# Two-layer recurrent and attention trunk on one core: norm factors found by token and spread by TensorE, a convolution that reads the accumulators, and another order of the work

## The chip, the core and the metric

The kernel runs on one core of a Trainium2 chip. The metric is the device time of one execution in microseconds (us). The kernel before took 615.57 us as the median of three runs (612.71, 615.57 and 615.72). One more execution was profiled; it took 608.61 us.

## The reference, cut to what matters

The input is a stream x of 256 tokens with 1024 features. Two layers each add a mixer and a feed-forward network to it, and a last norm follows. Everything is float32. Ahead of each product the stream is normed and then scaled and shifted by columns that come from the vector c:

```
rmsnorm(x, g) = x * rsqrt(mean(x*x over features) + 1e-6) * g
modulate(h, shift, scale) = h * (1 + scale) + shift        # shift, scale = silu(c) @ mod_w + mod_b
layer 0: x += g_m * rglru(h);       x += g_f * swiglu(h)
layer 1: x += g_m * attention(h);   x += g_f * swiglu(h)   # keys and values from a norm of their own
out = rmsnorm(x, final_norm)
```

The recurrent mixer (rglru) multiplies h by an input matrix, runs a causal convolution of four taps over the tokens of one half of the result, forms two gates from it, scans over the tokens, multiplies by a gelu of the other half and applies an output matrix. The convolution is

```
xc[t] = conv_b + sum over k = 0..3 of conv_w[k] * x_br[t - 3 + k]     # zero ahead of the first token
```

## The kernel before

Everything stands with features on the 128 partitions and the 256 tokens along the free axis, so the stream is eight tiles of 128 x 256. A float32 product is made in one of two ways. In the split way (`gemm`, `mm3`, L383 to L389) weights and data are each cut into a rounded high part and a low rest, and three matmuls replace one; ScalarE writes the high part of a weight unit (L439) and VectorE the low part (L440). In the native way the float32 tiles are multiplied as they are, and the profile has two records for each such matmul.

**Order of the work.** Nothing is ordered by a scheduler of the compiler. `build` writes down every operation with an estimated cost, a rank (its place in the text, plus a bias of the stage, plus a bias by tile name from the tables `PRIO`), and the buffers that it reads and writes. `Plan.run` (L153 to L265) walks through time with these estimates: on each engine the operations that could start earliest are found, and of those the one of lowest rank goes next. The order on each engine's queue is fixed by that, the loads on SP's queue too. On the chip each engine then works through its queue in order and waits on semaphores.

**Buffers.** Raw weights land in four `raw` slots of 1 MB. Rows of the modulation matrices (`mr_...`, 512 KB each) land in three `mraw` slots; VectorE reduces each such tile with the row csb, which is silu(c) spread over all partitions (`mod_col`, L458 to L463). PSUM has eight `ps` slots of one bank.

**The start.** c (`crow`) is loaded into an mraw slot, spread over the partitions by a matmul with ones (L422) and sent through silu into `csb` (L424). x, the vector constants `vec`, then the modulation rows and the slices `wix` of the input matrix (12 tiles of 128 columns a slice, 768 KB) follow on SP's queue. For each of the eight feature tiles k, VectorE makes the scale and the shift column (L462, L663, L666), multiplies x by the norm factor (`normed`, L555 to L558), ScalarE forms h (L563), and TensorE runs five native tiles (L677) and seven split tiles into the accumulators `xb0` to `xb4` and `yb0`.

**A norm** (`sumsq`, L522 to L553) is called four times: n0 ahead of the recurrent mixer, f0 and f1 ahead of the feed-forward networks, n2 ahead of keys, values and queries. ScalarE squares the eight tiles (L530) and VectorE adds some of them (L539). TensorE multiplies what is left by a matrix of ones (L544), so that each partition holds the sums of all tokens: one matmul in n0, five in each of the others. ScalarE takes the root of all 256 columns (L547) and VectorE the reciprocal of all 128 x 256 elements (L552). In f0, f1 and n2 the first products run on the stream before it is normed (`unnorm`, L585 to L603), and their results are multiplied by the factor afterwards (L879, L884, L988).

**The heads** (`head_front`, L695 to L739). For each of five heads ScalarE copies the accumulator `xb` into a zero-padded tile `xpad` (L699), writes the first tap (L705), and VectorE adds three more taps for each half (L709). Then the gates are made (`ga`, L725), with sigmoid, tanh, exp and root on ScalarE. `mod_cols_pe` (L465 to L497) makes the columns sh_f0 and g_m0 with TensorE from four loads each of 1 MB (`sh_f_r`, `g_m_r`, matmuls on L477). The keys are finished on VectorE (L990).

Of the kernel before, what the change touches and what calls it, by code (L numbers as in the profile page):

```python
# [92 lines left out]
class Plan:  # L93
# [59 lines left out]
    def run(self):  # L153
# [15 lines left out]
        te, table = {"ACT": 0.6, "DVE": 0.6, "POOL": 0.57, "PE": 0.1, "SP": 1.7}, [None]  # L169
# [102 lines left out]
    "shat": 0, "gmat": 1, "win": 600, "tol": 3.6321997149340305e-16, "nn": 5, "nyh": 1, "sqpe": 4, "gnat": 5,  # L272
# [5 lines left out]
        "cps": -877, "n_st": -1, "xb": 779, "yb": 1804, "ga": -19, "sh_f_ps": -1801, "sh_f_pt": 1118, "wo": -42,  # L278
        "g_m_ps": -799, "g_m_pt": -888, "f_st": 65, "f_g": 1113, "f_p": -3, "f_d": 23, "rp": 3432, "kp": -27, "vp":
        -23, "sp": -62, "pt": -29, "op": 1946, "ao": -145, "ty": 1267,  # L280
    },
    "ACT": {
        "csb": -187, "csc": -3, "n_sq": 1636, "n_rstd": 1867, "wix_h": -609, "h_": -1591, "h_h": -1809, "sp_e":
        -1313, "sp_ln": -1887, "xpad": 3698, "i": 1175, "v": 3772, "y": 3589, "wiy_h": 897, "sh_f_row": 473, "uh":
        -144, "wout_h": 2439, "g_m_row": -3, "f_warm": 1733, "f_sq": 8, "f_rstd": 458, "f_u_f": -2634, "f_": 54,
        "f_h": -427, "f_tg": 643, "f_ah": 1225, "fb_h": 3819, "f_s": 54, "fc_h": 15, "n_warm": 300, "kv_sh": 12,
        "wk_h": 785, "kv_u_h": -2508, "hkv_": 62, "hkv_h": -8, "hq_": 28, "hq_h": -2771, "wv_h": 3001, "v_": 4134,
        "wq_h": 2113, "qT": -1187, "sm": 4131, "e": -19, "pT": 132, "oh": 731, "wo__h": -26, "f_sh": -349, "fa_h":
        -75, "f_u_h": 619, "rs": 388, "out": -1641,
    },  # L290
    "DVE": {
        "epst": -623, "ones": 162, "n_sq": -421, "n_rstd": 796, "b": 2980, "sc": 15, "sh": 330, "wix_l": -577, "n_":
        396, "h_l": -2, "sp_neg": -45, "sp_ab": -1042, "sp_ln": 730, "sp_e": 357, "sp_d": -873, "sp_z": 171, "sp_s":
        -119, "xc": 4215, "i": -1135, "wiy_l": -1247, "r": 129, "v": -1006, "sh_f_m": 291, "y": 675, "ul": 1942,
# [24 lines left out]
def build(tc, t):  # L319
    nc = tc.nc  # L320
    ctx = ExitStack()
    with ctx:
# [914 lines left out]
```

## Time and profile before

| what | us |
|---|---|
| median of three runs | 615.57 |
| lowest and highest | 612.71, 615.72 |
| the profiled execution, its own time | 608.61 |
| its span, first to last instruction | 606.8 |
| TensorE busy in the span | 585.9 |
| VectorE busy | 471.8 |
| ScalarE busy | 340.6 |

The span is the part of an execution that the trace shows; 1.8 us of the profiled execution lie around it. All rows come from this one execution. A matmul's end is modelled, so two matmuls that follow each other overlap in the rows; the distance between two starts is what one costs.

### The profile page before, as it was taken

Reading aid. Unit: us, or ns where it says so; the run is one execution under the profiler, and the core shown is the slowest. Engines: PE = TensorE matmul, PEld = TensorE weight load, DVE = VectorE, ACT = ScalarE, POOL = GpSimd, SP = SyncE. Lnnn points to the kernel's source line nnn. Section 1 sums busy time; section 2 is a strip of 40 time slices with the busy share of each in tenths; the row PEclk is TensorE's granted clock in tenths of the full one; section 3 lists DMA queues with packets and bytes.
Section 4 is the critical chain, followed back from the end, with each engine's and each line's share of the span. In section 5 each row is a group of like instructions: output and inputs, shape, how many; then the busy total and the mean of one; then the engine's idle time right before and its main releaser. Section 6 shows DMA issues by size and latency. Waiting matters only on the chain.

```text
span 606.8 us, 11423 instructions
## 1 busy us (share of the span) xinstructions
PE 585.9 (97%) x4706; PEld 563.2 (93%) x4706; DVE 471.8 (78%) x743; ACT 340.6 (56%) x509; POOL 1.2 (0%) x10
## 2 busy tenths in 40 slices
PE   3999989999999999999999999998999999999996
PEld 1999868998999999999999889998999999999996
DVE  6998788977997898788878969889997654545542
ACT  6537898718653443343336899747664444434432
POOL 0000000000000000000000000000000000000000
PEclk9999999999999999999999999999999999999999
DMA  8996999795988899798979538786686654445501
GB/s 307 353 339 239 332 355 355 278 383 224 350 312 323 336 348 323 257 334 315 377 295 357 203 143 322 282 332 245 218 306 274 214 203 165 144 144 192 191 1 70
DMA packets 33362, 162.94 MB, mean 269 GB/s; under 512 B 3700, under 2 KB 4893, under 8 KB 23966
## 3 DMA queue, kind: packets, MB, share of 16 engines
q1 hardware_dynamic: 33310, 162.21, 72.2%
q8 instruction: 37, 0.61, 0.4%
q14 instruction: 15, 0.12, 0.1%
HBM read 161.14 MB, written 1.06 MB: 267 GB/s over the span
## 4 chain that ended last, share of the span: by engine, by line
PE 63%; DMA 18%; DVE 12%; ACT 3%; issue 3%; SPq 0%; DVEq 0%; ACTq 0%
PE ps_f_p L388 11%; PE ps_f_p L387 11%; PE ps_f_p L389 11%; PE ps_f_d L388 3%; PE ps_f_d L389 3%; PE ps_f_d L387 3%; PE ps_ga L449 3%; DMA mraw_mr_sh_kv_m__2730<-in_kvmod 2%; DVE wlo_f0c_l L440 2%; DMA raw_sh_f_r<-in_modp 1%; DMA mraw_mr_g_m_m__3469<-in_mod 1%; DMA raw_wix<-in_win_x 1%; PE ps_qp L389 1%; PE ps_qp L388 1%; PE ps_qp L387 1%
## 5 line engine op out<-in xcount | busy, mean ns | idle before, releaser
L388 PE MATMUL ps_f_p<-t_f_l,whi_f0b_h 128*128 128x256 f32 x320 | 89.7, 280 | 0.0
L387 PE MATMUL ps_f_p<-t_f_h,whi_f0b_h 128*128 128x256 f32 x320 | 89.5, 280 | 0.0
L389 PE MATMUL ps_f_p<-t_f_h,wlo_f0b_l 128*128 128x256 f32 x320 | 89.3, 279 | 0.0
L389 PE MATMUL ps_f_p<-t_f_h,wlo_f1b_l 128*128 128x256 f32 x320 | 88.5, 276 | 0.0
L387 PE MATMUL ps_f_p<-t_f_h,whi_f1b_h 128*128 128x256 f32 x320 | 88.4, 276 | 0.0
L388 PE MATMUL ps_f_p<-t_f_l,whi_f1b_h 128*128 128x256 f32 x320 | 88.4, 276 | 0.0
L388 PEld LDWEIGHTS ps_f_p<-t_f_l,whi_f0b_h 128*128 128x128 f32 x320 | 60.1, 188 | 0.2 <-DVE t_f_l L568 0.2
L387 PEld LDWEIGHTS ps_f_p<-t_f_h,whi_f0b_h 128*128 128x128 f32 x320 | 60.2, 188 | 0.0
L389 PEld LDWEIGHTS ps_f_p<-t_f_h,wlo_f1b_l 128*128 128x128 f32 x320 | 60.1, 188 | 0.1
L388 PEld LDWEIGHTS ps_f_p<-t_f_l,whi_f1b_h 128*128 128x128 f32 x320 | 60.1, 188 | 0.0
L387 PEld LDWEIGHTS ps_f_p<-t_f_h,whi_f1b_h 128*128 128x128 f32 x320 | 60.1, 188 | 0.0
L389 PEld LDWEIGHTS ps_f_p<-t_f_h,wlo_f0b_l 128*128 128x128 f32 x320 | 59.8, 187 | 0.0
L440 DVE TENSOR_TENSOR wlo_f1b_l<-raw_f1b_r,whi_f1b_h 128x2048 fp32r<-128x2048 f32 x20 | 45.6, 2289 | 18.1 <-ACT whi_f1b_h L439 18.1
L439 ACT ACTIVATE whi_f1b_h<-raw_f1b_r 128x2048 fp32r<-128x2048 f32 x20 | 38.2, 1912 | 24.8 <-issue 11.9
L439 ACT ACTIVATE whi_f0b_h<-raw_f0b_r 128x2048 fp32r<-128x2048 f32 x20 | 38.2, 1910 | 21.5 <-issue 19.1
L388 PE MATMUL ps_f_d<-t_f_al,whi_f0c_h 128*128 128x256 f32 x176 | 49.2, 280 | 0.8 <-DVE t_f_al L607 0.8
L389 PE MATMUL ps_f_d<-t_f_ah,wlo_f0c_l 128*128 128x256 f32 x176 | 49.3, 280 | 0.0
L387 PE MATMUL ps_f_d<-t_f_ah,whi_f0c_h 128*128 128x256 f32 x176 | 49.1, 279 | 0.0
L440 DVE TENSOR_TENSOR wlo_f0b_l<-raw_f0b_r,whi_f0b_h 128x2048 fp32r<-128x2048 f32 x20 | 45.6, 2287 | 4.2 <-ACT whi_f0b_h L439 4.1
L389 PE MATMUL ps_f_d<-t_f_ah,wlo_f1c_l 128*128 128x256 f32 x176 | 48.6, 276 | 0.0
L387 PE MATMUL ps_f_d<-t_f_ah,whi_f1c_h 128*128 128x256 f32 x176 | 48.6, 276 | 0.0
L388 PE MATMUL ps_f_d<-t_f_al,whi_f1c_h 128*128 128x256 f32 x176 | 48.6, 276 | 0.0
(469 smaller groups left out, 1661.3 us busy)
## 6 DMA issues: line engine op xcount, KB each, us to landing
raw_f0b_r<-in_ffb SPq DMA_DIRECT2D x20, 1024.0 KB, 6.9
raw_f1b_r<-in_ffb SPq DMA_DIRECT2D x20, 1024.0 KB, 4.9
raw_f0c_r<-in_ffc SPq DMA_DIRECT2D x16, 704.0 KB, 5.9
raw_f1c_r<-in_ffc SPq DMA_DIRECT2D x16, 704.0 KB, 4.0
raw_wix<-in_win_x SPq DMA_DIRECT2D x8, 768.0 KB, 6.7
raw_wout_r<-in_wout SPq DMA_DIRECT2D x5, 1024.0 KB, 9.9
raw_wiy_r<-in_win_y SPq DMA_DIRECT2D x4, 1024.0 KB, 6.0
raw_sh_f_r<-in_modp SPq DMA_DIRECT2D x4, 1024.0 KB, 6.1
```

What stands on the lines that cost most here:

```text
L387: nc.tensor.matmul(o, h_, a_, start=start, stop=False, skip_group_check=skip)
L388: nc.tensor.matmul(o, h_, b_, start=False, stop=False, skip_group_check=skip)
L389: nc.tensor.matmul(o, l_, a_, start=False, stop=stop, skip_group_check=skip)
L439: act(n - o, lambda: nc.scalar.activation(hi.ap[:, o:n], raw.ap[:, o:n], AF.Copy), (raw,), (hi,))
L440: tt(n - o, lambda: nc.vector.tensor_sub(lo.ap[:, o:n], raw.ap[:, o:n], hi.f[:, o:n]), (raw, hi), (lo,))
L449: pe(n * 0.0016875 + 0.002, lambda: nc.tensor.matmul(ps.ap[:, c:c + n], lo.ap[:, o:o + w], xh.ap[:, xo:xo + n], start=start, stop=stop, sk ...
```

## The change

- `sumsq` now adds the squares of tiles 0 to 4 on VectorE (0 to 5 in n0) and multiplies each sum or square by a single column of ones, with the squares as the stationary side, so that the sums stand with the tokens on the partitions, in two columns. Root and reciprocal work on 128 x 2 elements. Two matmuls with the identity spread the factors again, into the second half of the same PSUM bank. `normed` reads them from there; a copy in SBUF (by ScalarE) is made for the places where the other operand lies in PSUM too.
- The convolution reads the accumulator: ScalarE writes the last tap (unshifted), VectorE adds three shifted taps of 255, 254 and 253 columns. The copy into xpad and the memsets on GpSimd go.
- c is loaded straight into the first row of csb, not into an mraw slot.
- The first input slice comes in two transfers, 640 and 896 columns.
- The keys are finished on ScalarE instead of VectorE.
- All rank biases by name (`PRIO`) and the starting times of the engines in the plan are different, so the order on every queue is.

```diff
-        te, table = {"ACT": 0.6, "DVE": 0.6, "POOL": 0.57, "PE": 0.1, "SP": 1.7}, [None]
+        te, table = {"ACT": 0.7, "DVE": 0.7, "POOL": 0.57, "PE": 0.1, "SP": 0.6}, [None]
...
 PRIO = {
     "PE": {
...
-        "cps": -877, "n_st": -1, "xb": 779, "yb": 1804, "ga": -19, "sh_f_ps": -1801, "sh_f_pt": 1118, "wo": -42,
+        "cps": -2197, "n_st": 6219, "xb": -1551, "yb": 1853, "ga": -517, "sh_f_ps": 11, "sh_f_pt": 5023, "wo": 6470,
...
     "SP": {
-        "crow": -1540, "x_": -1004, "vec": 14, "mr_sc_": 3, "mr_sh_": -97, "wix": 21, "wga_r": -11, "wiy_r": 47,
-        "sh_f_r": -1282, "wout_r": 409, "g_m_r": -3732, "mr_sc_f_m_": 486, "fa_r": 3007, "fb_r": -446, "mr_g_f_m_":
...
+        "csb": -137, "x_": 4, "vec": -1083, "mr_sc_": -5, "mr_sh_": -3307, "wix": -7, "wga_r": 975, "wiy_r": -746,
+        "wout_r": -191, "mr_sc_f_m_": 389, "fa_r": 1968, "fb_r": 83, "mr_g_f_m_": 641, "mr_sc_kv_m_": 839,
...
-        crow = pl.buf("mraw", "crow")
-        load(crow, 8, lambda: crow.ap[0:1, :], t["c_row"])
+        load(csb, 8, lambda: csb.ap[0:1, :], t["c_row"])
...
-        def sumsq(xs, name, on_dve=False, prev=(), then=None):
+        def sumsq(xs, name, prev=(), then=None):
...
+                v = acc if k == adds else sq
+                for i in range(2):
+                    pe(0.235, lambda k=k, v=v, i=i: nc.tensor.matmul(
+                        st.ap[:, i:i + 1], v.ap[:, i * P:(i + 1) * P], ones.ap[:, 0:1], start=(k == adds and i == 0),
+                        stop=(k == KC - 1), skip_group_check=True), (ones, v), ((st, 0),))
+            rc = own([P, 2], f"{name}_rc")
+            act(2, lambda: nc.scalar.activation(rc.ap, st.ap[:, :2], AF.Sqrt, bias=epst.ap, scale=1.0 / D),
+                ((st, 0), epst), (rc,), AF.Sqrt, aps=1)
...
-            dve(S, 0.00628, lambda: nc.vector.reciprocal(r.ap[:, :S], r.ap[:, :S]), (r,), (r,))
-            return r
+            dve(2, 0.006, lambda: nc.vector.reciprocal(rc.ap, rc.ap), (rc,), (rc,))
+            for i in range(2):
+                pe(0.215, lambda i=i: nc.tensor.matmul(st.ap[:, S + i * P:S + (i + 1) * P],
+                                                       rc.ap[:, i:i + 1].to_broadcast([P, P]), ident.ap, start=True,
+                                                       stop=True, skip_group_check=True), (rc, ident), ((st, 1 + i),))
+            rs = Half(st, S)
+            if then is None:
+                return rs, None
+            r = T1(f"{name}_rstd")
+            act(S, lambda: nc.scalar.activation(r.ap[:, :S], rs.ap, AF.Copy), ((st, 1), (st, 2)), (r,))
+            return rs, r
...
+            if k == 0:
+                load((wr, 0), NN * P, lambda wr=wr: wr.ap[:, :NN * P], t["win_x"][k][:, :NN * P])
+                load((wr, 1), (nt - NN) * P, lambda wr=wr: wr.ap[:, NN * P:nt * P], t["win_x"][k][:, NN * P:])
...
-            act(2 * S, lambda: nc.scalar.activation(
-                xv()[:, :, 3:], xps[h].ap.rearrange("p (a b) -> p a b", a=2), AF.Copy), (xps[h],), (xp,))
...
+                act(S, lambda m=m, o=o: nc.scalar.activation(
+                    x_.ap[:, o:o + S], xps[h].ap[:, o:o + S], AF.Identity, bias=V("cb", m), scale=V("cw", 30 + m)),
+                    (xps[h], vec), ((x_, o),), aps=2)
+                for d in range(1, 4):
+                    stt(S - d, lambda m=m, o=o, d=d: nc.vector.scalar_tensor_tensor(
+                        x_.ap[:, o + d:o + S], xps[h].ap[:, o:o + S - d], V("cw", (3 - d) * 10 + m),
+                        x_.ap[:, o + d:o + S], op0=OP.mult, op1=OP.add), (xps[h], vec, (x_, o)), ((x_, o),))
...
-            ts(S, lambda m=m, tk=tk: nc.vector.tensor_scalar(kT[m // 2].ap[:, (m % 2) * S:(m % 2 + 1) * S],
+            act(S, lambda m=m, tk=tk: nc.scalar.activation(kT[m // 2].ap[:, (m % 2) * S:(m % 2 + 1) * S], tk.ap[:, :S],
+                                                           AF.Identity, bias=bk.ap[:, m:m + 1]),
```

## Rows read from the trace of the kernel before

**Rows 1.** The page: busy time, share of the span and instructions of each engine.
```profile
PE 585.9 (97%) x4706; PEld 563.2 (93%) x4706; DVE 471.8 (78%) x743; ACT 340.6 (56%) x509; POOL 1.2 (0%) x10
```
**Rows 2.** Waits of TensorE in the whole span: us in total, times, longest.
```profile
PE ps_xb L677 <- ACT t_h L563: 4.7, 2, 4.4
...
PE ps_f_st L544 <- DVE t_f_sq L539: 2.3, 2, 2.1
PE ps_sh_f_ps L477 <- DMA raw_sh_f_r<-in_modp: 2.2, 1, 2.2
PE ps_kp L388 <- DVE t_kv_u_l L601: 0.9, 1, 0.9
PE ps_f_d L388 <- DVE t_f_al L607: 0.8, 1, 0.8
```
**Rows 3.** Two stretches: length, busy (instructions) by engine, granted clock, DMA share, GB/s.
```profile
160.00:200.00 40.00, 40.00 (x342) 40.00 (x341) 33.55 (x44) 20.84 (x19) 0.00 (x0) 1.00 0.87 317
480.00:520.00 40.00, 40.00 (x356) 40.00 (x355) 21.38 (x15) 18.61 (x15) 0.00 (x0) 1.00 0.51 182
```
**Rows 4.** Timeline of TensorE at 434 us: start, us, what.
```profile
434.11 0.28 PE L388 MATMUL ps_f_p<-t_f_l,whi_f1b_h 128*128 128x256 f32 x1
434.31 0.38 PE L389 MATMUL ps_f_p<-t_f_h,wlo_f1b_l 128*128 128x256 f32 x1
```
**Rows 5.** Timeline of the start, 8 to 15 us.
```profile
8.60 1.22 PE L544 MATMUL ps_n_st<-t_n_sq,ones 128*128 128x256 f32 x2 [2.52 <-DVE t_n_sq L539]
...
10.18 1.22 DVE L462 SCALAR_TENSOR_TENSOR mraw_mr_sh__250<-mraw_mr_sh__250,csb 128x1024 f32<-128x1024 f32 x1
...
11.32 1.75 DVE L552 RECIPROCAL t_n_rstd<-t_n_rstd 128x256 f32<-128x256 f32 x1
...
12.09 0.95 ACT L439 ACTIVATE whi_wix_h<-raw_wix 128x896 fp32r<-128x896 f32 x1 [1.76 <-DMA raw_wix<-in_win_x]
...
13.57 0.60 ACT L563 ACTIVATE t_h<-t_n,sh,sc 128x256 f32<-128x256 f32 x1 [0.53 <-DVE t_n L557]
...
14.22 4.63 PE L677 MATMUL ps_xb<-t_h,raw_wix 128*128 128x256 f32 x10 [4.41 <-ACT t_h L563]
```
**Rows 6.** Groups by form: copies and short operations.
```profile
L699 ACT ACTIVATE xpad<-ps_xb 128x512 f32<-128x512 f32 x5 | 2.9, 596 | 0.0
...
L1133 DVE RECIPROCAL rs<-rs 128x2 f32<-128x2 f32 x1 | 0.2, 165 | 1.1 <-ACT rs L1131 1.1
```
**Rows 7.** Timeline of TensorE at the f0 norm and at the end.
```profile
135.14 7.63 PE L449 MATMUL ps_f_g<-t_f_u_f,raw_f0a_r 128*128 128x258 f32 x34
142.97 2.42 PE L544 MATMUL ps_f_st<-t_f_sq,ones 128*128 128x256 f32 x10 [0.20 <-DVE t_f_sq L539]
145.23 4.95 PE L449 MATMUL ps_f_g<-t_f_u_f,raw_f0a_r 128*128 128x258 f32 x22
...
598.76 0.50 PE L1121 MATMUL ps_n_st<-ones,t_n_sq 128*128 128x1 f32 x4
599.12 0.96 PE L1125 MATMUL ps_ty<-ident,t_y 128*128 128x128 f32 x7
```
**Rows 8.** Timeline, sixth input slice.
```profile
38.81 0.95 ACT L439 ACTIVATE whi_wix_h<-raw_wix 128x896 fp32r<-128x896 f32 x1 [3.96 <-DMA raw_wix<-in_win_x]
...
40.30 2.43 PE L677 MATMUL ps_xb<-t_h,raw_wix 128*128 128x256 f32 x10 [0.26 <-ACT t_h L563]
```
**Rows 9.** The stretch of the input product, columns as in rows 3.
```profile
20.00:50.00 30.00, 29.72 (x200) 27.75 (x199) 26.90 (x77) 13.03 (x21) 0.00 (x0) 1.00 0.94 349
```
**Rows 10.** Groups by form: busy us, mean ns | idle before.
```profile
L709 DVE SCALAR_TENSOR_TENSOR t_xc<-xpad,vec,t_xc 128x256 f32<-128x256 f32 x30 | 12.8, 481 | 0.8 <-ACT t_xc L705 0.6
...
L611 DVE SCALAR_TENSOR_TENSOR t_x<-ps_wo,g_m_m,t_x 128x256 f32<-128x256 f32 x8 | 3.4, 478 | 0.0
```
**Rows 11.** Timeline of VectorE and TensorE at the first heads.
```profile
52.39 5.34 DVE L709 SCALAR_TENSOR_TENSOR t_xc<-xpad,vec,t_xc 128x256 f32<-128x256 f32 x13
...
54.81 7.07 PE L449 MATMUL ps_ga<-t_xc,raw_wga_r 128*128 128x256 f32 x32
```

More of the change, by code (lines that the diff above doesn't have):

```diff
@@ L281 @@
+        -111, "qp": 1872, "sp": 79, "pt": -136, "op": 8787, "ao": 744, "ty": 7136,
     },
     "ACT": {
[L283 to L286, printed above, removed]
@@ L311 @@
+        "rows": 100, "G": -2467, "wk_r": -546, "wv_r": 604, "mr_g_m_m_": -1625, "wq_r": -5, "mr_sh_f_m_": -18,
+        "wo__r": -32, "out": -888,
     },
@@ L421, in build @@
             c = slice(i * 512, (i + 1) * 512)
-            pe(0.86, lambda cps=cps, c=c: nc.tensor.matmul(cps.ap, ones.ap[0:1, :], crow.ap[0:1, c], start=True,
-                                                           stop=True), (ones, crow), (cps,))
+            pe(0.86, lambda cps=cps, c=c: nc.tensor.matmul(cps.ap, ones.ap[0:1, :], csb.ap[0:1, c], start=True,
+                                                           stop=True), (ones, (csb, i)), (cps,))
             silu.append(act(512, lambda cps=cps, c=c: nc.scalar.activation(csb.ap[:, c], cps.ap, AF.Silu), (cps,),
@@ L526, in sumsq @@
             st = PS(f"{name}_st")
-            acc, parts = None, []
+            acc, adds = None, KN["n0adds" if name == "n0" else "adds"]
             for k in range(KC):
@@ L531, in sumsq @@
                     (sq,))
[L532 removed]
+                if k == 0:
                     acc = sq
[L534 to L548 removed]
+                elif k <= adds:
+                    tt(S, lambda sq=sq: nc.vector.tensor_add(acc.ap[:, :S], acc.ap[:, :S], sq.ap[:, :S]), (acc, sq),
+                       (acc,))
+                if k < adds:
+                    continue
+                v = acc if k == adds else sq
[6 more added lines that the diff above has]
+                ((st, 0), epst), (rc,), AF.Sqrt, aps=1)
             last = pl.ops[-1]
@@ L686, in build @@
         xc, rr_, ii, vv_, ys = [], [], [], [], []
-        xpad = []
-        for i in range(3):
-            b = own([P, 2 * (S + 3)], f"xpad{i}")
-            gp(6, 0.01, lambda b=b: nc.gpsimd.memset(b.ap.rearrange("p (a b) -> p a b", a=2)[:, :, :3], 0.0), (), (b,))
-            xpad.append(b)
         after = []
@@ L703, in head_front @@
                 m = 2 * h + j
-                o = slice(j * S, (j + 1) * S)
-                act(S, lambda m=m, j=j, o=o: nc.scalar.activation(
-                    x_.ap[:, o], xv()[:, j, 0:S], AF.Identity, bias=V("cb", m), scale=V("cw", m)), (xp, vec),
-                    ((x_, j * S),), aps=2)
-                for tap in range(1, 4):
-                    stt(S, lambda m=m, j=j, o=o, tap=tap: nc.vector.scalar_tensor_tensor(
-                        x_.ap[:, o], xv()[:, j, tap:tap + S], V("cw", tap * 10 + m), x_.ap[:, o], op0=OP.mult,
-                        op1=OP.add), (xp, vec, (x_, j * S)), ((x_, j * S),))
+                o = j * S
+                act(S, lambda m=m, o=o: nc.scalar.activation(
[5 more added lines that the diff above has]
+                        x_.ap[:, o + d:o + S], op0=OP.mult, op1=OP.add), (xps[h], vec, (x_, o)), ((x_, o),))
             gnat = h < KN["gnat"]
```

85 lines of the change are left out of this document (35 added, 50 removed).

## The prediction

> **What bounds the kernel now.** I read the busy times first: TensorE works in 585.9 of 606.8 us, VectorE in 471.8, ScalarE in 340.6 [rows 1]. So the time is that of TensorE's queue, and another engine counts only where TensorE waits for it. The second view is the list of TensorE's waits [rows 2]. Before the first large product, which starts at 14.22 us, it is idle or busy with small things. After that it stands still five times: 0.3 us in the input product (4.7 less the 4.4 of the start), 2.2 us for a load of sh_f0, 2.3 us in two places for the squares of a norm, and 0.9 and 0.8 us for low parts that VectorE makes. That is 6.5 us; together with the start it is all that a change of order or of small operations can win, apart from what it takes off TensorE's own work.
>
> The third view is TensorE's pace. [...] The pace changes within one stage, at 434 us, where two starts are 0.20 us apart [rows 4] instead of the usual 0.12 (40 us by 342). At the first pace the 165 us of dense matmuls from 434 us to the end of the products would take 165 x 356 / 342 = 171.8 us, so this execution would have taken 608.6 + 6.8 = 615.4 us. That is the median of the runs (615.57) and its neighbour (615.72). I take it that most executions keep the slower pace and that the profiled one is 7 us better for this reason alone. The sum below holds differences only, and I set it against the median.
>
> **The start.** The norm's last matmul starts at 8.60 us. Its reciprocal of 128 x 256 elements has to let two modulation reductions pass on VectorE, the second from 10.18 to 11.40 us, and then takes 1.75 us to 13.07; n, h and the first product follow at 14.22 us [rows 5]. In the new kernel the reciprocal is that of two columns, 0.165 us [rows 6]. Two matmuls that spread the factors are added. A native matmul of 256 columns costs two records of 0.226 us ((145.23 - 142.97) / 10 [rows 7]), so one of 128 columns costs about 0.23 us, and both 0.45; but the first ten records of the input product took 4.63 us [rows 5] and later ones 2.43 [rows 8], so at this point I double it: 0.9 us. If the reciprocal goes ahead of the second reduction, the spreading lies beside that reduction, and the product follows n (0.50 us from 13.07 to 13.57 before) and h (0.65 to 14.22) at about 11.40 + 0.50 + 0.65 = 12.6 us. If it goes behind, add 0.17 + 0.9: 13.6 us. The weights must be there too: the slice landed at 12.09 us [rows 5] as a whole, and the first piece of it comes earlier. The one more issue on SP's queue, and vec and c ahead of x, cost some tenths that lie beside the reductions. So the start gains 0.6 to 1.6 us.
>
> Not all of it lasts. At the sixth slice ScalarE waited 3.96 us for the weights and TensorE 0.26 us behind it [rows 8]: there the products have caught up with the transfers. From 20 to 50 us the DMA engines are busy for 0.94 of the time and VectorE for 26.9 of 30 us [rows 9]. The transfers can win at most 0.06 x 30 = 1.8 us, and their mraw slots come free when VectorE gets to them. VectorE has 1.75 - 0.17 = 1.6 us less to do ahead of this. That c no longer holds an mraw slot lets one load issue earlier, into a queue that is full. I take **-1.0 us**, between 0 and -1.6.
>
> **The other norms.** In f0 the first products on the unnormed stream run from 135.14 us, ahead of the sums (142.97) and behind them (145.23) [rows 7]. Root, reciprocal and spreading lie beside these products; nothing on TensorE waits for a factor [rows 2]. So the shorter reciprocal is worth nothing there by itself. If the cover goes, it is worth 1.6 us a norm. On TensorE five matmuls (2.26 us) become eight of one column and two that spread. Four records of one column took 599.12 - 598.76 = 0.36 us [rows 7]; sixteen take 1.44, with 0.45 for the spreading 1.9: -0.4 us a norm. At the usual 0.12 us a matmul they take 1.9 + 0.45, which is +0.1. I take **-0.5 us** for the three, between -1.2 and +0.3. In n0 TensorE is idle anyway.
>
> **The waits.** The sh_f0 matmuls move back by 1800 ranks in TensorE's table and their loads lose their place ahead on SP. They then run behind the heads' other products, and sh_f0 is first read by the products at 135 us. I take all of that wait: **-2.2 us** (0 at worst, if the loads come late again behind the wout loads that they now follow). The norm and low-part waits (2.3 + 0.9 + 0.8 = 4.0) are not touched by any edit but the order; f1's squares come in another grouping, and VectorE, which is late there, has less to do. I let half go: **-2.0 us**, between 0 and -4.0. A new order over the whole kernel will also have waits of its own: **+1.5 us**, the mean of the four waits after the first [rows 2], between 0 and their sum of 6.2.
>
> **The convolution, the keys and the rest.** ScalarE loses five copies of 0.596 us [rows 6], VectorE the xpad wait of 0.8 us in all [rows 10]. The three taps read PSUM instead of SBUF. A multiply-add of this form out of PSUM takes 478 ns, the present one from SBUF 481 [rows 10]: no difference, and three columns fewer at most. [...] On VectorE four reciprocals go (6.3 us) and the key operations move to ScalarE. All this is beside TensorE, which hides it; where it moved a wait, it is in the two numbers above.
>
> **The sum.** -1.0 - 0.5 - 2.2 - 2.0 + 1.5 = -4.2 us: 615.6 - 4.2 = **611.4 us**; an execution of the profiled kind would take 604.4. The bounds added up are -9.0 and +6.5.
>
> **Rivals.** (A) *The gain is hidden.* The start is given back at the sixth slice, and the new order waits as long as the old one. Three of the four norms are off the path already, so for them the change does nothing of what it says. Left is -0.5: 615.1 us. For it: [rows 8, 9], and that only a quarter of the sum comes from the edits themselves. Against it: the sh_f0 wait is one of order alone and its matmuls have plenty of time.
>
> (B) *Slower: the accumulators are held.* Before, a head's bank was free after a copy of 0.60 us; now it is free after six taps, which VectorE does at 5.34 / 13 = 0.41 us each [rows 11], 2.5 us a head. Six of the eight banks hold xb and yb, and a head's gates want two. If TensorE waits for this at each of the four later heads, it costs 4 x (2.5 - 0.6) = 7.6 us, and the time is 611.4 + 7.6 = 619.0 us. It turns to slower by over 0.5% when all four waits come in full. [...] Against it: two banks are free all along, the gates of two heads take 7.07 us in one piece [rows 11], more than the taps of two heads, and the output tiles yb can go between.
>
> (C) *The pace.* If most runs change to the faster pace early, as the profiled one did, the same kernel takes 604.4 us. It says nothing of the change, but it moves the result.
>
> **Chances.** Forecast 0.50, with a range of its own of 609 to 614; A 0.22; B 0.12; C 0.16. A measurement of this kernel can tell about 0.5% from no change, which is 3.1 us: faster is under 612.5, slower over 618.7. Of the forecast, three quarters lie under 612.5, the rest within. Faster: 0.37 + 0.16 = 0.53; within: 0.13 + 0.22 = 0.35; slower 0.12. The range reaches from C's 604 to 617.5, which leaves out most of B and the rare cases beyond C.
>
> **What would show it.** Right: the first native input product starts at 12.6 to 13.6 us; no wait for raw_sh_f_r on TensorE; the one-column sums with a tenth of a microsecond a record; no new wait over 2 us. The sixth slice shows what lasts of the start: if TensorE waits there for more than 1 us, A's first half is true. Wrong: waits of TensorE at the gates for taps (B), or a list of waits as long as before (A). A pace of 356 matmuls in 40 us from early on is C.

## The result, and the profile after

The changed kernel takes 619.27 us as the median of 20 runs, the kernel before 614.30 as the median of 20 on the same chip. The ratio is 1.0107, with a 95% interval of 1.0065 to 1.0149. The prediction was 611.4 and faster; the change is slower by 5 us. Some executions of either kernel run over 1.5% longer than its fastest one; all ratios and clocks below leave these out, and the medians keep them.

The page of the kernel after answers to [rows 1]:

```profile
span 615.6 us, 11522 instructions
...
PE 597.7 (97%) x4750; PEld 575.9 (94%) x4750; DVE 466.8 (76%) x740; ACT 338.4 (55%) x511; POOL 1.1 (0%) x7
...
PEclk9999999999999999999999999998999999999999
```

TensorE is busy for 97% as before, VectorE 5 us less, ScalarE 2 us less. What the edits took off the two side engines shows there, and nothing of it reached the end. The waits of TensorE after (waiting line, what ended the wait: us in total, times, longest) answer to [rows 2]:

```profile
PE ps_cps L421 <- DMA csb<-in_c_row: 2.8, 1, 2.8
PE ps_f_d L389 <- DVE wlo_f0c_l L439: 2.3, 2, 1.2
PE ps_n_st L541 <- DVE t_n_sq L535: 1.6, 1, 1.6
PE ps_xb L688 <- ACT t_h L570: 1.6, 2, 1.1
PE ps_ga L448 <- DMA raw_wga_r<-in_wg: 1.4, 1, 1.4
PE ps_f_st L541 <- DVE t_f_sq L535: 1.0, 1, 1.0
PE ps_n_st L552 <- DVE sh L677: 0.8, 1, 0.8
PE ps_sh_f_ps L476 <- DMA raw_sh_f_r<-in_modp: 0.5, 1, 0.5
PE ps_f_d L387 <- ACT whi_f0c_h L438: 0.4, 1, 0.4
```

The old waits are shorter, as forecast: the 4.4 us of the start, the 2.2 us for sh_f0, the low parts. Two are new: 1.4 us for the gate weights, and 2.7 us in layer 0's down projection (`f_d`, weights `f0c`). From the first large product on, TensorE's waits add up to 6.1 us, against 6.4 before: the list has changed and is as long. Around the second new wait the clock falls too. The windows of TensorE in that stretch (start and end, length, busy time and instructions, granted clock, DMA share, GB/s):

```profile
300.00:302.00 2.00, 0.84 (x7) 1.00 0.96 359
302.00:304.00 2.00, 2.00 (x20) 1.00 0.97 390
304.00:306.00 2.00, 1.59 (x14) 1.00 1.06 368
306.00:308.00 2.00, 0.85 (x5) 0.86 0.99 400
308.00:310.00 2.00, 2.00 (x11) 0.50 1.07 397
```

TensorE waits, works, waits again, and then runs at half speed, at a granted clock of 0.50 (11 matmuls from 308 to 310 us, 20 from 302 to 304 us at 1.00), until 310.8 us. It does so once more after layer 1's norm. The one-column sums and a wait of 1.0 us came just before:

```profile
416.00:418.00 2.00, 1.04 (x9) 1.00 0.09 37
418.00:420.00 2.00, 2.00 (x20) 1.00 0.03 8
420.00:422.00 2.00, 2.00 (x12) 0.52 0.17 37
422.00:424.00 2.00, 2.00 (x13) 0.63 0.92 365
```

In windows of 0.1 us the two half-speed stretches last from 307.4 to 310.8 us and from 420.1 to 423.5 us. At a clock of 1.00 in the place of 0.50 the work of these 6.8 us would have taken half as long, so as an estimate they cost about 3.4 us. This theory came first: the loss is layer 0's down projection and the clock. The rival: the loss is spread, and the two profiles differ by the pace of [rows 3].

### The profile page after: what moved, and what is told of

It reads as the page before. It is cut to its first block, busy times and chain, and to the rows that moved or that the text cites. A ratio compares the mean times of both kernels' runs of the same rounds, so it can differ in the third digit from the quotient of the medians.

```text
span 615.6 us, 11522 instructions
## 1 busy us (share of the span) xinstructions
PE 597.7 (97%) x4750; PEld 575.9 (94%) x4750; DVE 466.8 (76%) x740; ACT 338.4 (55%) x511; POOL 1.1 (0%) x7
## 4 chain that ended last, share of the span: by engine, by line
PE 62%; DMA 16%; DVE 12%; ACT 5%; issue 4%; SPq 1%; DVEq 0%; ACTq 0%
PE ps_f_p L387 7%; PE ps_f_p L389 7%; PE ps_f_p L388 7%; PE ps_f_d L389 5%; PE ps_f_d L387 5%; PE ps_f_d L388 4%; DMA raw_f0c_r<-in_ffc 2%; PE ps_f_g L448 2%; DVE wlo_f0b_l L439 2%; PE ps_wo L388 2%; PE ps_wo L387 2%; PE ps_wo L389 2%; DMA mraw_mr_g_f_m__2173<-in_mod 1%; DMA mraw_mr_sh_m_m__3084<-in_mod 1%; DMA mraw_mr_g_f_m__2034<-in_mod 1%
```

## The experiments

All results stand in one table. The ratio is to the kernel before, run on the same chip in the same set of runs. "Clock" is the mean granted clock over the runs that the ratio counts; a value lower by 0.001 is 1.2 us more at half speed, which costs 0.6 us. The last four columns come from the one profile of each run: us from the start to the first product of layer 0's down projection, from there to the first score product, from there to the last product of the attention output, and from there to the last matmul.

| run | median us | ratio (95%) | clock | to f_d | to scores | to ao's end | to the end |
|---|---|---|---|---|---|---|---|
| before | 614.2 (141 runs) | 1 | 0.996 to 0.997 | 265.0 | 94.9 | 53.7 | 188.0 |
| again_before | 614.38 | 1.0011 (0.9954 to 1.0068) | 0.997 | 265.5 | 93.5 | 53.5 | 192.8 |
| after | 619.27 | 1.0107 (1.0065 to 1.0149) | 0.994 | 264.3 | 97.3 | 54.0 | 194.9 |
| again_after | 620.40 | 1.0167 (1.0075 to 1.0258) | 0.992 | 267.9 | 97.9 | 54.0 | 194.9 |
| e1 | 659.67 | 1.0714 (1.0663 to 1.0764) | 0.960 | | | | |
| e2 | 642.36 | 1.0434 (1.0388 to 1.0481) | 0.984 | | | | |
| e3 | 627.68 | 1.0206 (1.0164 to 1.0248) | 0.986 | | | | |
| e4 | 631.55 | 1.0269 (1.0213 to 1.0325) | 0.990 | | | | |
| g1 | 619.93 | 1.0070 (1.0031 to 1.0108) | 0.990 | 263.1 | 100.5 | 55.8 | 197.3 |
| g2 | 618.86 | 1.0062 (1.0023 to 1.0100) | 0.998 | 268.3 | 93.4 | 53.5 | 194.8 |
| g3 | 621.63 | 1.0123 (1.0078 to 1.0167) | 0.989 | 266.1 | 100.9 | 53.8 | 194.9 |
| g4 | 618.25 | 1.0061 (1.0032 to 1.0090) | 0.997 | 265.5 | 94.9 | 53.3 | 195.0 |
| h_conv | 613.33 | 1.0018 (0.9975 to 1.0062) | 0.997 | 268.6 | 92.7 | 53.9 | 187.5 |
| h_start | 615.02 | 1.0064 (1.0021 to 1.0107) | 0.995 | 265.9 | 94.1 | 53.8 | 194.3 |
| h_norms | 622.29 | 1.0146 (1.0075 to 1.0216) | 0.988 | 272.4 | 97.6 | 53.4 | 197.5 |
| h_kt | 615.77 | 1.0025 (0.9977 to 1.0074) | 0.997 | 265.5 | 95.7 | 54.6 | 193.0 |
| k1 | 611.44 | 0.9978 (0.9944 to 1.0012) | 0.995 | 265.0 | 91.8 | 54.0 | 193.4 |
| k2 | 609.58 | 0.9948 (0.9893 to 1.0003) | 0.997 | 267.0 | 92.8 | 54.8 | 192.7 |
| k3 | 611.09 | 0.9931 (0.9899 to 0.9964) | 0.995 | 265.2 | 92.7 | 54.7 | 192.7 |
| k4 | 615.60 | 1.0024 (0.9993 to 1.0056) | 0.996 | 264.1 | 94.0 | 53.5 | 196.9 |

The profiled executions of g1, h_norms and k2 are among the longest of their runs (623.55, 627.91 and 614.27 us), so their last four columns show what happens and overstate how much.

### First set: priorities exchanged

**e1**: the changed kernel with the priorities and start times of the kernel before; **e2** the other way round. In each, a name that the borrowed priorities lack gets the number of the operation that it replaces; for e1:

```diff
+PRIO['SP']['csb'] = PRIO['SP']['crow']
+for e in ('ACT', 'DVE'):
+    PRIO[e]['n_rc'], PRIO[e]['f_rc'] = PRIO[e]['n_rstd'], PRIO[e]['f_rstd']
+PRIO['ACT']['kT'] = PRIO['DVE']['kT']
```

> All edits of the change, the planner keeping the old priorities and start times. Order theory (the loss is layer 0's down projection, whose weight loads the new order puts behind modulation loads, about 6 us there): the down projection takes about 62 us as before, not 67.9, and the time falls to 611 to 615 us. Edit theory (one-column sums and the accumulators held for the convolution cost the time): 617 to 620 us, with the clock falling after the norms' one-column products. Pace theory (5 us are the spread of matmul pitch between runs, 113 against 118 ns): the time goes with this run's pitch, whatever the stages show.

> None of the edits, but the new priorities and start times (the old names get the keys of the new ones). Order theory: the down projection of layer 0 starves as in the changed kernel (66 us or more, TensorE waiting for layer 0's third weights near 300 us) and the time is 617 to 621 us. Edit theory: 613 to 616 us, the same as before the change, down projection near 62 us.

**e3**: six loading priorities put back.

```diff
+PRIO['SP'].update({'fc_r': -3000, 'mr_sh_kv_': -1225, 'mr_sc_m_': -205, 'mr_sc_m_m_': -205, 'mr_sh_m_m_': -409, 'mr_g_m_m_': -289})
```

> The changed kernel with six loading priorities put back (layer 0's third weights and the modulation loads beside them): 14 of the 16 weight loads then come before the last group of modulation loads, 8 in the changed kernel, 12 before the change. Order theory: the waits and the clock fall near 300 to 311 us go, that stage gives back 4 to 6 us, the time is 613 to 615 us. Edit theory: stage and time move by under 1.5 us, 618 to 620 us. If the second theory of the stage holds (what is won there is lost as a wait in the attention stage, which in the changed kernel ran 3.6 us shorter), the stage wins 4 to 6 us and the time only 1 to 2.

**e4**: the old way to the norm factors.

```diff
-                for i in range(2):
-                    pe(0.235, lambda k=k, v=v, i=i: nc.tensor.matmul(
-                        st.ap[:, i:i + 1], v.ap[:, i * P:(i + 1) * P], ones.ap[:, 0:1], ...
...
+                pe(0.43, lambda v=v, i=i: nc.tensor.matmul(st.ap[:, :S], ones.ap, v.ap[:, :S], ...
```

> The changed kernel with the old norm: sums of 256 columns against ones, root and reciprocal over 256 columns, no spreading. Edit theory in its form for the norms (one-column products let the clock fall, 1.7 us at layer 1's norm): the granted clock stays at full speed from 416 to 425 us, and with the other norms the time falls to 614 to 616 us. Order theory: the time stays at 618 to 621 us, up to 2 us worse for the longer reciprocal.

Measured: 659.7, 642.4, 627.7 and 631.6 us. All four missed every theory. The reason is the instrument. The planner places each operation by a simulated clock, so any edit moves places all over the kernel. In e3, where only six numbers changed, a new wait of 8.0 us stands at the norm ahead of the keys. Such a run tests a plan that nobody chose. What these four runs show is that the priorities and the list of operations fit each other: changing one of them alone cost 12 to 44 us by the medians.

### Second set: the order written out

From here on the choice of the next operation is replaced. `PLACE` holds the place that each operation has in the order of one of the two kernels; new operations stand where those they replace stood. With its own list of operations each kernel would keep its order.

```diff
         left = len(ops)
+        place = {o: PLACE[i] for i, o in enumerate(ops)}
         while left:
             best = None
-            for eng, lst in pend.items():
...
+            for o in sorted((o for lst in pend.values() for o in lst), key=place.get):
+                s = slot_time(o)
+                if s is not None:
+                    best = (max(o.ready, s, te.get(o.eng, 0.0)), o)
+                    break
```

**g1**: the changed kernel's operations in the old order. **g2**: the old operations in the new order.

> All edits of the change, but with every engine's instructions in the order that the kernel before has them, written down place by place instead of planned (the new instructions stand where the ones they replace stood). Order theory (the edits are harmless, the new order costs the time): 610 to 614 us, down projection of layer 0 62 us. Edit theory (one-column sums and held accumulators): 617 to 621 us in this order too. Pair theory (edits and order only work together, as the two kernels with borrowed priorities, 660 and 642 us, may say): 617 us or more, with new waits at the norms, because the old order puts too little work between the sums and the spread factors.

> None of the edits, every engine's instructions in the changed kernel's order. Order theory: 618 to 622 us, TensorE starving by 3 us and the clock falling near 300 to 311 us, as in the changed kernel. Edit theory: 613 to 616 us. Pair theory: over 622 us, with the convolution or the norms late for their place in the order.

**g3**: the changed kernel; the f0c loads and splits and the modulation loads and reductions around them in the old order among themselves.

The table `PLACE` of g3 holds the outcome of the lines below, which are not in its kernel; `new` and `old` give the place of every operation in the two orders. In g3's trace the loads of f0c and of these rows stand in SP's queue one for one as in the kernel before.

```diff
+NEAR = re.compile(r"f0c\d+_|(mr_)?(sc_m1|sh_m1|g_m1|sh_kv)_m")
+moved = [k for k in new if k in old and k[0] in ("SP", "DVE", "ACT") and NEAR.match(k[1])]
+new.update(zip(sorted(moved, key=old.get), sorted(new[k] for k in moved)))
```

> The changed kernel with TensorE's order untouched; only layer 0's third weights (loads and splits) and the modulation loads around them change places among themselves, into the order of the kernel before: 12 of 16 weight loads come before the last group of modulation loads, 8 in the changed kernel. Order theory: the starving at 300 to 311 us goes, the down projection takes 62 to 63 us and not 67.9, and the time falls by 3 to 6 us to 613 to 616. If what is won there is lost again in the attention stage, the stage falls as much but the time by under 1.5 us. Edit theory: neither moves by over 1 us.

**g4**: the old way to the norm factors as in e4, with the changed kernel's order; VectorE also adds the squares that it adds in the changed kernel, so four products of 256 columns are left in a later norm, where e4 has the five of the kernel before.

> The changed kernel, order untouched, with the old way to the norm factors: products of 256 columns against ones, root and reciprocal over 256 columns, no spreading and no copy. Edit theory for the norms (the clock falls after the one-column products, 1.7 us at layer 1): no fall at 416 to 425 us, time 615 to 618 us. If the new sums gain as the prediction had it (0.5 us at the norms, 2 us at the start from the short reciprocal): 620 to 623 us, the first product near 16 us. Order theory alone: 618 to 621 us.

Measured: 619.9, 618.9, 621.6 and 618.3 us. So the old order with the edits is as slow as the new order without them. No theory fits both: g1 lies in the ranges of the edit and the pair theory; g2 lies in that of the order theory, but without the starving that it named. In g1 the clock carries most of it: 0.990 against 0.996 is 3.7 us of work lost, and the loss by the ratio is 4.3. g2 and g4 have no wait for f0c and no fall of the clock in their profiles and are still 4 to 5 us up. g3 shows the transfer that its expectation named as the second outcome, though the time rises where a small gain was named: the stage loses its wait for f0c, but TensorE waits 4.8 us, in two pieces, for the squares of the next norm, and from the start of the second piece the clock is at half speed:

```profile
338.00:340.00 2.00, 1.65 (x7) 0.50 0.98 401
340.00:342.00 2.00, 2.00 (x12) 0.50 1.04 430
```

From the down projection to the scores g3 takes 100.9 us, more than the changed kernel. Exchanging two streams of loads changed what waits there and did not end the waiting; what delays the squares is not shown.

### Third set: twins, and single edits

**again_before** and **again_after** are the two kernels once more, with no edit.

> The kernel before once more, for a second profile. Pace theory (the matmul pitch falls from 118 to 113 ns in stretches that come by chance): another profile shows the 113 ns stretch in another place or not at all, and stages of the same order differ by 1 to 3 us between two profiles of one kernel. If the quick second half belongs to this kernel, the pitch falls at about 434 us again. Ratio to the kernel before 1.00, within its interval.

> The changed kernel once more, for a second profile. If the starving of TensorE near 300 us is a property of its order, it stands there again (2 to 4 us of waits for layer 0's third weights, down projection 66 us or more); if it was one execution's delay, the down projection takes 62 to 63 us, as in the two kernels that have the same order and not all edits, and the 5 us must lie elsewhere. 617 to 621 us.

The twin of the kernel before keeps the slower pace to its end (342 matmuls in 480 to 520 us):

```profile
480.00:520.00 40.00, 40.00 (x342) 1.00 0.48 169
```

Its last part takes 192.8 us against 188.0, and its runs have a median of 614.4. So the quick second half of [rows 3] is an event of one execution. The twin of the changed kernel waits for f0c again, 3.3 us, and its clock falls at the same two places (308.3 to 311.7 and 424.3 to 427.7 us). That is a property of the kernel, in two profiles of two. The twin of before also lets the two kernels be compared at the same pace. The spans of the changed kernel's first profile and of the twin of before are 615.6 and 610.4 us, 5.2 apart: waits after the first large product 6.1 against 4.5, 3.4 us lost to half speed against none, and a start 0.4 us sooner leave 0.6 us unexplained.

**h_conv** is the old order with the convolution's edit alone, **h_start** with the first norm's, c's place and the two transfers alone. These diffs, and those of h_norms and h_kt, are against the kernel before.

```diff
-                for tap in range(1, 4):
-                    stt(S, lambda m=m, j=j, o=o, tap=tap: nc.vector.scalar_tensor_tensor(
-                        x_.ap[:, o], xv()[:, j, tap:tap + S], V("cw", tap * 10 + m), x_.ap[:, o], ...
+                for d in range(1, 4):
+                    stt(S - d, lambda m=m, o=o, d=d: nc.vector.scalar_tensor_tensor(
+                        x_.ap[:, o + d:o + S], xps[h].ap[:, o:o + S - d], V("cw", (3 - d) * 10 + m), ...
```

```diff
-        load(crow, 8, lambda: crow.ap[0:1, :], t["c_row"])
+        load(csb, 8, lambda: csb.ap[0:1, :], t["c_row"])
...
+        def sumsq(xs, name, prev=(), then=None):
+            return (sumsq_new if name in ('n0',) else sumsq_old)(xs, name, prev=prev, then=then)
```

> The kernel before, every engine's order as it was, with the convolution reading the accumulators and nothing else of the change. Edit theory with the convolution as its cause (accumulators held longer: the gates' and the next heads' products wait for a place): 617 to 620 us and 2 to 4 us more between the first gate product and the output projection. If the convolution is harmless or a gain, as predicted: 613 to 615 us.

> The kernel before, order as it was, with the first norm by tokens, the place for c and the two transfers of the first weights, and nothing else. As predicted: the first product 0.5 to 1.5 us sooner and the 4.4 us wait for the second h shrinks to about 1, time 611 to 614 us. If the start's gain is given back before the gates because the loads set that stage: 614 us. Edit theory: 615 us or more.

The convolution shows no cost: 1.0018 (0.9975 to 1.0062). The start gains where it was said to. The first product starts at 13.57 us and the first gate product at 53.3 (54.8 before), but the output projection starts at 107.2 us, as in the two profiles of before (106.9 and 107.2). The gain is gone before layer 0's norm. TensorE waits 2.3 us ahead of the sh_f0 products, as before (2.2), but here the clock is at half speed for 3.4 us behind that wait, which costs 1.7 us, about what had been won. The time is no better: 1.0064, whose interval of 1.0021 to 1.0107 leaves out a gain.

### Fourth set: the later norms, the keys, one more buffer

**h_norms** is the old order with the new sums in f0, n2 and f1 only; **h_kt** with the keys' bias on ScalarE only.

```diff
+            return (sumsq_new if name in ('f0', 'n2', 'f1') else sumsq_old)(xs, name, prev=prev, then=then)
```

```diff
-            ts(S, lambda m=m, tk=tk: nc.vector.tensor_scalar(kT[m // 2].ap[:, (m % 2) * S:(m % 2 + 1) * S], ...
+            act(S, lambda m=m, tk=tk: nc.scalar.activation(kT[m // 2].ap[:, (m % 2) * S:(m % 2 + 1) * S], ...
```

> The kernel before, order as it was, with the three later norms (layer 0's, the one before the keys, layer 1's) by one-column sums, short root and reciprocal, spreading and copy, and nothing else. Edit theory for the norms: most of what all edits cost in this order (6 us) is here, 617 to 620 us, in the stretch from layer 0's down projection to the scores (94 us before, 100.5 with all edits) or as a clock fall after the one-column products. As predicted (gain 0.5 us): 613 to 614.5 us, that stretch 93 to 95 us.

> The kernel before, order as it was, with the keys' bias added by ScalarE and nothing else. If that edit is the costly one (ScalarE then makes the keys between the exponentials): 616 to 620 us, 3 us or more after the key products. If it is as small as predicted: 613 to 615 us.

The keys show no cost either (1.0025). The new sums cost 9 us by the ratio (1.0146) and 7 by the medians (622.3 against 615.3). No wait of that size stands in their profile; the clock shows it. The norms ahead of the keys and of layer 1's feed-forward network on TensorE's timeline (start, us, what, and in brackets the idle time before), then the windows there:

```profile
340.28 1.95 PE L623 MATMUL ps_n_st<-ones,t_n_sq 128*128 128x1 f32 x16
...
425.40 0.39 PE L436 MATMUL ps_f_g<-t_f_u_l,whi_f1a_h 128*128 128x258 f32 x1 [1.12 <-DVE t_f_u_l L693]
426.96 2.66 PE L623 MATMUL ps_f_st<-ones,t_f_sq 128*128 128x1 f32 x16
```

```profile
340.00:344.00 4.00, 3.94 (x24) 0.83 0.56 199
344.00:348.00 4.00, 4.00 (x19) 0.50 0.60 240
348.00:352.00 4.00, 4.00 (x30) 0.81 0.02 3
...
428.00:430.00 2.00, 2.00 (x11) 0.50 0.70 281
432.00:434.00 2.00, 2.00 (x11) 0.50 0.83 348
434.00:436.00 2.00, 2.00 (x15) 0.79 0.00 0
```

The twin of the kernel before, in the same order, with the 2.3 us of 256-column sums ahead of the keys in the place of one-column ones:

```profile
332.48 2.33 PE L544 MATMUL ps_n_st<-t_n_sq,ones 128*128 128x256 f32 x10
```

```profile
333.00:337.00 4.00, 4.00 (x23) 1.00 0.67 213
337.00:341.00 4.00, 4.00 (x36) 1.00 0.39 159
```

The two kernels differ in the three norms alone. TensorE counts as busy with either kind of sum, but with the one-column products it runs at half speed for 6.8 us right behind them ahead of the keys, and for 6.8 us from the middle of them at layer 1, where a wait of 1.1 us comes before. (A third fall of 6.8 us, from 79.8 us, goes with a wait of 3.1 us for a load and has no norm near it.) Over the runs of h_norms the mean clock is 0.988, against 0.997 before: 0.009 of 620 us is 5.6 us of work lost, most of the loss, with the third fall counted in. (The time lies above the 617 to 620 us of the expectation.) The waits alone do not do it: h_start waits 1.1 us and h_kt 1.9 us shortly before the 256-column sums ahead of the keys, and before waits 2.1 us at those of layer 1, all without a fall. Nor do the sums do it each time: at layer 1's norm five of the six profiles with one-column sums have a fall (k1 has none) and one of the ten with 256 columns (k4); ahead of the keys g1 and both profiles of the changed kernel have one-column sums and no fall. Nor do single prices add up: the four edits one by one give 1.0018, 1.0064, 1.0146 and 1.0025, and together in the same order (g1) only 1.0070 (1.0031 to 1.0108).

**k1** is the changed kernel, in its own order, with a fourth buffer for modulation rows; **k2** is h_conv with the same (the convolution's edit frees the room).

```diff
-T1N, T2N, RAWN, WN, MRN = 18, KN["t2n"], KN["rawn"], KN["wn"], 3
+T1N, T2N, RAWN, WN, MRN = 18, KN["t2n"], KN["rawn"], KN["wn"], 4
```

> The changed kernel, every engine's order untouched, with four buffers for modulation rows in the place of three, so that the loading queue is held less by VectorE's release of such a buffer and the weight loads queued behind go out sooner. Margin theory (the new order leaves layer 0's third weights no lead over TensorE, which takes one every 3.8 us: the tenth is split 34 to 36 us after the down projection begins, 24.5 in the kernel before): the tenth is split by 30 us, the starving and the clock fall near 300 us go, the stretch to the scores falls from 97.5 to 94 us and the time to 615 to 617. If the DMA engines and not the queue set these loads (share 0.9 to 1.0 there): under 1 us, 618.5 to 620.5.

> The kernel before with the convolution from the accumulators (which frees the room) and four buffers for modulation rows, order as it was. The old order has 10 us of lead there, so margin theory gives no gain in the down projection: 612 to 614.5 us. If loads queued behind modulation rows hold other stages too (the output projection's, the shift rows' at 77 us): 609 to 612 us.

k1 takes 611.4 us where the changed kernel takes 619.3: 0.9978 to the kernel before, against 1.0107. No instruction changed its place in a queue; the loads only go out sooner. In the changed kernel SP's queue stands for VectorE's release of a modulation buffer 13 times between 262 and 300 us, 0.3 to 3.5 us each and 25.9 us in all (once, for 0.3 us, in the kernel before). Two of these waits (what ended them: us in total, times, longest), then its queue (start, us, what):

```profile
SPq L381 <- DVE mraw_mr_g_m_m__3278 L461: 3.5, 1, 3.5
SPq L381 <- DVE mraw_mr_sh_m_m__3204 L461: 2.9, 1, 2.9
```

```profile
280.88 0.33 SPq L381 DMA_DIRECT2D mraw_mr_sh_m_m__3204<-in_mod  x1
285.21 0.33 SPq L381 DMA_DIRECT2D mraw_mr_g_m_m__3238<-in_mod  x1
285.63 1.27 SPq L381 DMA_DIRECT2D raw_f0c_r<-in_ffc  x1
```

and the same three in k1:

```profile
273.39 0.33 SPq L429 DMA_DIRECT2D mraw_mr_sh_m_m__3205<-in_mod  x1
278.75 0.33 SPq L429 DMA_DIRECT2D mraw_mr_g_m_m__3239<-in_mod  x1
279.17 0.38 SPq L429 DMA_DIRECT2D raw_f0c_r<-in_ffc  x1
```

These weights, the ninth of f0c's sixteen loads, go out 6.5 us sooner, though the down projection begins 0.6 us later; the tenth go out at 291.45 and 285.40 us. What that does to the lead over TensorE shows in the tenth split of f0c by ScalarE. In the changed kernel the projection's first product and that split stand at

```profile
264.34 0.39 PE L387 MATMUL ps_f_d<-t_f_ah,whi_f0c_h 128*128 128x256 f32 x1
...
298.29 1.38 ACT L438 ACTIVATE whi_f0c_h<-raw_f0c_r 128x1408 fp32r<-128x1408 f32 x1 [3.73 <-DMA raw_f0c_r<-in_ffc]
```

34.0 us apart; in k1

```profile
264.98 0.39 PE L435 MATMUL ps_f_d<-t_f_ah,whi_f0c_h 128*128 128x256 f32 x1
...
291.20 1.38 ACT L486 ACTIVATE whi_f0c_h<-raw_f0c_r 128x1408 fp32r<-128x1408 f32 x1 [1.25 <-DMA raw_f0c_r<-in_ffc]
```

26.2 us, and in the two profiles of before 24.5 and 23.5. With nothing to wait for, the sixteen last 62.3 us in k1, 3.9 us each, so TensorE needs the tenth 9 x 3.9 = 35 us after the first, and the low part of it still has to be made. With 34.0 (36.2 in the twin) there is no lead; with 26.2 there are 9 us. k1's windows have no gap and no fall:

```profile
300.00:304.00 4.00, 4.00 (x36) 1.00 0.98 356
304.00:308.00 4.00, 4.00 (x36) 1.00 0.69 229
```

The margin theory holds in its mechanism: the starving and the fall at 300 us go and the tenth split comes sooner. The gain is larger than it said, 611.4 us where it had 615 to 617; in the profile the fall at layer 1's norm is gone too. The DMA engines, busy for 0.82 to 1.00 of the time, in windows of 8 us, from 264 to 304 us in the changed kernel, still let the loads come sooner in k1 (0.91 to 1.01). k2 seems to gain as well, 609.6 us against 615.3 by the medians, but its ratio of 0.9948 reaches 1.0003; so whether the old order was held too is not certain from k2.

### Fifth set: is that all of it

**k3** is k2 with five buffers (`MRN` 5). **k4** is k1 with the old sums in the three later norms.

```diff
+            return (sumsq_new if name in ('n0',) else sumsq_old)(xs, name, prev=prev, then=then)
```

> The kernel before with the convolution from the accumulators and five buffers for modulation rows, order as it was. If the hold of the loading queue by these buffers is the limit that four of them eased (615.3 to 609.6 us), a fifth gives 1 to 3 us more, 606 to 609. If four already cover it: 609 to 611 us, no difference.

> The changed kernel with four buffers for modulation rows, as before, but the three later norms with the old sums of 256 columns and the long reciprocal; order untouched, the first norm stays new. If the one-column sums still cost time once the loads have their lead (clock falls at the norms): 608 to 610.5 us, against 611.4 with them. If they cost only where TensorE has little else queued behind them, which in the new order it has (the run with four buffers showed no clock fall at layer 1's norm): 611 to 613 us, the 256-column products costing their 1 us at each norm.

k3 takes 611.1 us, on a chip where the kernel before takes 613.8: 0.9931 (0.9899 to 0.9964). With five buffers the gain of the old order is certain; that the fifth adds nothing to the fourth fits the two ratios and is not shown. By its ratio k3 beats both kernels. k4 is 1.0024, and k1 with the new sums 0.9978; their intervals overlap, so no more can be said than that no harm of the new sums shows once the loads have their lead. That is the direction of the second outcome of its expectation, but 615.6 us lies outside both ranges. Its profile gives part of the reason: TensorE waits 2.1 us at layer 1's norm and 1.5 us at the key products, and the clock falls at that norm.

## Why the prediction was wrong

**The step that failed** is the term of the new order's waits, "+1.5, between 0 and 6.2", with no term beside it for the clock. The new waits measured 4.1 us in one profile of the changed kernel and 5.1 in the other, where 1.5 was taken, and half speed behind them and at layer 1's norm took another 3.4 us in each. The main cause is that, in the new order, the modulation rows hold the queue that the weights f0c also wait in; k1, with a fourth buffer for these rows, showed it: 611.4 us against 619.3.

**The start, -1.0.** The gain came in part and did not last. h_start's first product comes at 13.57 us, just inside 12.6 to 13.6, by the case in which the reciprocal runs behind the second reduction. In the changed kernel the product comes at 14.00 us, outside that range and 0.2 us ahead of [rows 5]: the four records of spreading take 1.19 us where the prediction had 0.9:

```profile
11.66 1.19 PE L552 MATMUL ps_n_st<-ident,n_rc 128*128 128x128 f32 x4 [0.78 <-DVE sh L677]
14.00 4.04 PE L688 MATMUL ps_xb<-t_h,raw_wix 128*128 128x256 f32 x10 [1.15 <-ACT t_h L570]
```

Nothing of h_start's gain is left at 107 us, as rival A had it. That the transfers take it back, as [rows 8, 9] suggest, is not shown: TensorE has no wait over 1 us at the sixth slice in h_start or in the first profile of the changed kernel.

**The other norms, -0.5.** Wrong in sign by a cost that was not in the sum at all. I weighed the durations of records on TensorE, and these gave no gain either: sixteen records took 1.95 us and the spreading 0.6, against 2.3 before. The runs showed that with the one-column sums the clock is lower: 9 us in the old order (h_norms); in the new order 3.4 us at half speed at layer 1's norm, which cost 1.7. The trace of before could not show it: its sums in these norms are 256 columns wide, and its one-column records at the end [rows 7] have no dense products behind them.

**The waits.** The sh_f0 wait shrank from 2.2 to 0.5 us, but TensorE now waits 1.4 us for the gate weights (1.8 in the twin, for a low part of other weights; what delays them is not shown). Of the other waits more went than the half I took. The new waits are where the sum failed: "+1.5, between 0 and 6.2" was a mean of the old waits, taken in place of reading the new loading priorities. These move the modulation rows ahead of f0c by thousands of ranks, and with three buffers the rows held the queue for 25.9 of the 38 us from 262 to 300 us. On TensorE this measured 2.7 and 3.3 us of waits in the two profiles, and 3.4 us at half speed behind them in each, of which half is lost. The waits lie inside the bound; the half speed behind them had no term. The stretch from the down projection to the scores became 97.3 and 97.9 us from 94.9 and 93.5, and 91.8 with a fourth buffer. With that buffer, and the order untouched, the loss is gone (k1), and 5.5 of the 6.3 us between the spans of the two profiles are won in this stretch; so this term is the main error.

**The convolution and the keys, nothing.** Right as far as these runs can tell, which is some 4 us: 1.0018 (0.9975 to 1.0062) and 1.0025 (0.9977 to 1.0074). The taps after, which read PSUM, take 470 to 472 ns as a mean each for 253 to 255 columns, against 481 for 256 columns from SBUF before: no cost of that reading shows.

**The rivals.** A is right in its list of waits, as long as before (6.1 and 6.4 us); its 615.1 us leaves out the half speed. Its "only a quarter of the sum" is a quarter of the gains of 5.7 us and over a third of the sum of 4.2. B named 619.0 us, which is what came, by luck: TensorE's list has no wait of the gates for taps, and with the held accumulators alone (h_conv) no loss shows. C's pace is real but belongs to executions: the changed kernel's two profiles run at 342 matmuls in 40 us in both stretches of [rows 3]; the second one, in the first profile:

```profile
480.00:520.00 40.00, 40.00 (x342) 1.00 0.51 182
```

**What stays open.** g2 and g4 have the new order, the old sums and no starving in their one profile, and are still 1.006. In the tenth split they stand between (29.9 and 31.3 us). Their profiles show other waits after the first large product, 6.2 and 7.8 us against 4.5 in the twin of before; in g4 these 3.3 us are nearly the difference of the spans (613.8 and 610.4 us): the largest are 1.8 us for a square ahead of the keys, 1.7 us at the gates and 2.7 us at layer 1's norm, all for VectorE or ScalarE. So the new order costs something with the old sums that is not the starving, and that the hold of the loads is behind it is not shown. In g2 over 2 us stay unexplained. In k4 the clock fell for 3.4 us at layer 1's norm although its sums there have 256 columns, and in k1 it did not although they have one. So the falls here go with a wait, with one-column sums or with both, and what decides between a fall and none is not shown. How much of the fourth buffer's gain the old order would have too is open as well.

## What to carry to other kernels

Here one queue carried two streams, and the weights f0c had to wait where the modulation rows waited for buffers: a fourth buffer sent the ninth load of f0c out 6.5 us sooner. With such a queue, ask of each new order how many microseconds every load lands before its use, and look for a buffer before looking for a better order. Read the clock around a small operation, not only its own time: norms with fewer columns on TensorE were forecast cheaper by the record and were 9 us dearer by the run, at a mean clock of 0.988 against 0.997. An order that was tuned for one list of operations says little of an edit; to price an edit, keep the order place by place and change the edit alone, and measure the edits together as well, since here the single prices did not add up.

## What was not expected of the hardware

In these profiles TensorE's dense products run at one of two paces at an unchanged granted clock of 1.00, 342 or 355 to 356 matmuls in 40 us. h_conv takes the quick one in the same stretch as [rows 3], and g1 in layer 0, though not later (342 matmuls in 480 to 520 us):

```profile
160.00:200.00 40.00, 40.00 (x342) 1.00 0.88 323
480.00:520.00 40.00, 40.00 (x355) 1.00 0.51 177
```

```profile
180.00:220.00 40.00, 40.00 (x355) 1.00 0.89 332
```

The last part of the kernel is 4.8 us shorter with the quick stretch (188.0 against 192.8), although before waits 1.7 us longer there; from the first `f_p` product of layer 1 to the last of its down projection the two take 170.0 and 176.4 us. Nothing in the traces says what starts it. It makes single profiles of one kernel differ by as much as this whole change, so a single profile of this kernel should not be read to 5 us.
